# First loads by k-tile, the residual stream later, and a smaller-grained end in a two-layer fp32 trunk on one NeuronCore

## The chip, the cores and the metric

The kernel runs on one core of a Trainium2 chip. The metric is the device time in microseconds (us), lower is better. A run of the profiler gives, beside it, a trace of one execution; TensorE appears there as PE (matmuls) and PEld (weight loads), VectorE as DVE, ScalarE as ACT, GpSimd as POOL, SyncE, which issues most DMAs, as SP.

## The reference

Two layers over 256 tokens of width 1024, all in fp32. Cut to what matters:

```python
def rms_norm(x, g):
    return x * lax.rsqrt(jnp.mean(x * x, axis=-1, keepdims=True) + 1e-6) * g

def swiglu(x, w_in, w_out):                  # w_in 1024 x 5632, w_out 2816 x 1024
    gate, up = jnp.split(x @ w_in, 2, axis=-1)
    return (jax.nn.silu(gate) * up) @ w_out

h = x                                        # 256 x 1024
for i in range(2):
    h = h + 0.5 * swiglu(rms_norm(h, ffn_norm[i, 0]), ffn_w_in[i, 0], ffn_w_out[i, 0])
    u = rms_norm(h, mix_norm[i])
    h = h + (mla_mixer(u) if i == 0 else fox_mixer(u))
    h = h + 0.5 * swiglu(rms_norm(h, ffn_norm[i, 1]), ffn_w_in[i, 1], ffn_w_out[i, 1])
    gate = jax.nn.sigmoid(rms_norm(h, ple_norm[i]) @ ple_w_gate[i])
    h = h + gate * (p[i] @ ple_w_proj[i])
return rms_norm(h, final_norm)
```

## The kernel before

The residual stream lies in SBUF transposed, as `hT`: 8 k-tiles of 128 features by 256 tokens, in one tile `state` together with all norm gains (`g_sb`). Every weight and every activation that goes into a large product is split into a high part (rounded to fp32r) and a low part (the rest): ACT makes the high part (`whi`, lines 98 and 275), DVE the low part (`wlo`, lines 102 and 280). A product is then three fp32r products, hi·hi, hi·lo and lo·hi; `part` does them per k-tile with one matmul of 512 columns (both activation parts, line 236) and one of 256 (the low weights, line 237), `mm3` with three equal ones (lines 221 to 223), which is the form with the activations as the stationary operand.

`Weights` streams the weights in a fixed plan, in rows of 128 x 1024: a DMA on SP into one of four `raw` buffers, ACT and DVE into one of seven `whi`/`wlo` pairs, then PE. `pump` splits the next one and lets SP fetch into the buffer that this frees. All engines run their instructions in the written order.

RMSNorm is deferred: PE multiplies the gained but unnormalised stream, and the reciprocal root (`rtok`, on POOL, line 310, from `v` on DVE, line 308) is spread over the partitions by a small matmul (`by_column`, lines 315 and 318) and multiplied in when the product leaves PSUM (line 329). In the first FFN the sum of squares comes from a token-major copy of x, `tokens` (line 958 on ACT). There `ffn` puts `by_token` after the gate block of c = 2 and `by_column` after its up block; PE therefore takes the `pb` matmuls between the up block of c = 2 and the gate block of c = 3.

The start: SP loads `state` in three pieces (2, 2 and 4 k-tiles) alternating with four slabs of 128 x 1024 that hold the weights of the first two gate and up blocks, two k-tiles each; then two `raw`, the two halves of `tokens`, and two more `raw`. PE meanwhile runs 22 matmuls on zeros (`cold`). ACT and DVE split each k-tile's stream and weights in turn, and `first` multiplies k-tile by k-tile into four PSUM banks, each bank's 512-column matmul followed by its 256-column one.

The end is `ple_by_token`: the last gated embedding with tokens on the partitions, so that the final norm needs no transpose. For each of two token tiles t, two half rows of 512. The first halves of both are done together; then t = 0's second half (512), then t = 1's in two parts of 256 columns. After each part `gated` does sigmoid (ACT), two products and a sum (DVE), a square with row sum (ACT), and the product with the final gain (DVE, line 847). `store` adds the sums (853), scales and adds eps (854), takes the power on POOL (855), scales the row in two halves (858 ACT, 860 DVE) and stores them (861).

Of the kernel before, what the change touches and what calls it, by code (L numbers as in the profile page):

```python
# [60 lines left out]
class Weights:  # L61
# [20 lines left out]
    def take(self, raws):  # L82

        self.raws.update(enumerate(raws))
        self.fetched = self.ahead = len(raws)
# [56 lines left out]
def trunk(ctx, tc, xT, xt, pT, pos, freq, bf, ffn_first, ffn_in, ffn_out, w_down, w_uq, w_ukv, mla_o,  # L142
# [13 lines left out]
    def plan_ffn(i):  # L156

        plan.extend(ffn_first[k] for k in range(0 if i else KD // 2))
# [103 lines left out]
    class Norm:  # L262


        def __init__(self, gain, blocks, dim, tag="u"):
            self.gain, self.dim, self.acc, self.sums = gain, dim, None, None
            self.pair = act.tile([P, blocks, 2, T], F32R, name=tag, bufs=2 if tag == "u" else 1)

        def high(self, b, src, vector=False, cuts=(slice(0, T),)):
            g = g_sb[:, self.gain + b:self.gain + b + 1]  # L270
            for c in cuts:
                if vector:
                    nc.vector.tensor_scalar(self.pair[:, b, 0, c], src[:, c], g, None, op0=ALU.mult)
                else:
                    nc.scalar.activation(self.pair[:, b, 0, c], src[:, c], AF.Copy, scale=g)  # L275

        def low(self, b, src, cuts=(slice(0, T),)):
            g = g_sb[:, self.gain + b:self.gain + b + 1]
# [43 lines left out]
    def ffn(norm, nxt, then=None, first=None, meanwhile=None, later=None):  # L322
# [23 lines left out]
        def up(c, ps, pumps=1):  # L346
# [480 lines left out]
    def ple_by_token(pp, norm):  # L827
# [6 lines left out]
        sums = work.tile([P, 2, 3], F32, name="sums", bufs=1)  # L834
# [5 lines left out]
        def gated(t, ps, a, i):  # L840
# [5 lines left out]
            nc.scalar.activation(sg, h[:, t, a], AF.Square, accum_out=sums[:, t, i:i + 1])  # L846
            nc.vector.tensor_mul(es[:, t, a], h[:, t, a], gain[:, a])

        def store(t, n):
            s = work.tile([P, 1], F32, name="s")  # L850
            v = work.tile([P, 1], F32, name="v1")
            r = work.tile([P, 1], F32, name="r")
            nc.vector.reduce_sum(s, sums[:, t, :n], axis=AX.X)
            nc.vector.tensor_scalar(v, s, 1.0 / D, EPS, op0=ALU.mult, op1=ALU.add)
            nc.gpsimd.tensor_tensor(r, v, mhalf[:, :1], op=ALU.pow)
            for i, a in enumerate(half):
                if t and i == 0:
# [39 lines left out]
        for t in range(2):  # L897

            cuts = [half[1]] if t == 0 else [slice(N, N + N // 2), slice(N + N // 2, D)]
            for i, a in enumerate(cuts):  # L900
                last = bank("ps", (P, a.stop - a.start))
                for k in range(KD):
                    b = (k % 2 - 1) * N
                    rows(last, ws[k // 2], norm.pair, k, slice(a.start + b, a.stop + b), t, KD - 1)
                gated(t, last, a, 1 + i)
                if (t, i) == (1, 0):
                    store(0, 2)
        store(1, 3)
# [3 lines left out]
    n0 = Norm(G_FFN, KD, D)  # L912
    slabs = big.tile([P, KD // 2 + 2, D], F32, name="slabs", tag="big")
    tokens = slabs[:, KD // 2:, :]
    W.take([slabs[:, i, :] for i in range(KD // 2)])

    a = 0
    for i, n in enumerate((2, 2, 4, 0)):
        if n:
            b = GAINS + (2, 4, 8)[i] * T  # L920
            nc.sync.dma_start(state[:, a:b], xT[:, a:b])
            a = b
        nc.sync.dma_start(slabs[:, i, :], ffn_first[i])
# [4 lines left out]
    W.fetch()  # L928

# [3 lines left out]
    for _ in range(22):  # L933
        nc.tensor.matmul(cold, warm[:, :P], warm, start=True, stop=True)
    half = [slice(0, 4 * P), slice(4 * P, 8 * P)]
    for k in range(KD):
        if k % 2 == 0:
            W.pair()
        n0.high(k, hT[:, k, :])
        W.high(k // 2, half[k % 2])  # L940
        n0.low(k, hT[:, k, :])
        W.low(k // 2, half[k % 2])
# [3 lines left out]
    def first(ps):  # L946
        for k in range(0, KD, 2):
            w, = W.get()
            for j in range(2):
                for i, p in enumerate(ps):  # L950
                    part(p, w, n0.pair, range(k + j, k + j + 1), KD - 1, at=lambda x: (j * 4 + i) * P)
            W.done(w)
            W.pump()
            if k == 0:
# [143 lines left out]
def _layout(x, p, positions, ffn_norm, ffn_w_in, ffn_w_out, mix_norm, mla_w_down, mla_q_norm, mla_w_uq,  # L1098
# [58 lines left out]
_ORDER = ["xT", "xt", "pT", "pos", "freq", "bf", "ffn_first", "ffn_in", "ffn_out", "w_down", "w_uq", "w_ukv", "mla_o",  # L1157
# [22 lines left out]
```

## Time and profile before

| | us |
|---|---|
| median of 3 runs | 1001.4 (1001.32 to 1002.94) |
| the profiled execution | 1001.46 |
| its span, first to last instruction | 999.7 |
| PE busy in it | 988.8 (99%) |
| DVE, ACT, POOL busy | 740.5, 517.6, 423.7 |

Between the span and the time of the same execution lie 1001.46 - 999.7 = 1.8 us that no instruction shows. PE is busy for all but 11 us, so what is of interest is where those 11 us lie and what releases PE there. In the stretch from 24 to 960 us PE is busy for 934.5 of 936; the rest is in the first 24 us and in the 7.9 us after the last matmul.

### The profile page before, as it was taken

How to read it: one execution, taken by the hardware profiler on the slowest of the kernel's cores; microseconds unless marked ns; L12 is line 12 of the kernel's file. 1: busy time of each engine (PE TensorE's matmuls, PEld its weight loads, DVE VectorE, ACT ScalarE, POOL GpSimd, SP SyncE). 2: the span in 40 equal slices, each digit the busy share in tenths (PEclk: the TensorE clock that was granted, in tenths of full speed). 3: DMA queues.
4: the chain of work that ended last, by engine and by line, in shares of the span. 5: the costliest groups of instructions: out<-in, count | busy, mean ns of one | idle time of the engine just before them, and what ended most of it. 6: DMA issues, size and time to landing. Idle time of an engine off the chain costs nothing.

```text
span 999.7 us, 16018 instructions
## 1 busy us (share of the span) xinstructions
PE 988.8 (99%) x5940; PEld 875.1 (88%) x5940; DVE 740.5 (74%) x1051; ACT 517.6 (52%) x825; POOL 423.7 (42%) x348
## 2 busy tenths in 40 slices
PE   9999999999999999999999999999999999999996
PEld 7888888998988888889888888899889888888886
DVE  5777879676768787667778876666777778876674
ACT  7555444456655544555555444546445554544552
POOL 0777730110267775111477673211221577671120
PEclk9999999999999999999999999999999999999999
DMA  8566666651456666665366656666443566666561
GB/s 330 177 209 208 190 181 191 187 169 53 132 182 207 189 190 185 193 196 195 127 198 206 192 182 192 180 194 206 151 142 102 189 202 199 189 179 201 178 210 43
DMA packets 51388, 180.54 MB, mean 181 GB/s; under 512 B 5872, under 2 KB 6000, under 8 KB 51312
## 3 DMA queue, kind: packets, MB, share of 16 engines
q1 hardware_dynamic: 50880, 178.75, 57.3%
q8 instruction: 47, 0.77, 0.3%
q10 hardware_dynamic: 432, 0.79, 0.3%
q14 instruction: 29, 0.24, 0.1%
HBM read 178.46 MB, written 1.05 MB: 180 GB/s over the span
## 4 chain that ended last, share of the span: by engine, by line
PE 91%; DVE 4%; ACT 2%; issue 1%; POOL 0%; DMA 0%; POOLq 0%; SPq 0%; ACTq 0%; DVEq 0%
PE pu L236 16%; PE po L236 16%; PE pg L236 16%; PE po L237 8%; PE pu L237 8%; PE pg L237 8%; PE ps L236 4%; PE ps L237 2%; DVE wlo L102 1%; PE ps L221 1%; PE ps L223 1%; PE ps L222 1%; PE pv L221 1%; PE pv L223 1%; PE pv L222 1%
## 5 line engine op out<-in xcount | busy, mean ns | idle before, releaser
L102 DVE TENSOR_TENSOR wlo<-raw,whi 128x1024 fp32r<-128x1024 f32 (+2 forms) x338 | 416.8, 1241 | 17.8 <-ACT whi L98 17.1
L98 ACT ACTIVATE whi<-raw 128x1024 fp32r<-128x1024 f32 (+2 forms) x338 | 336.4, 1027 | 20.9 <-DMA raw<-in_ffn_in_dram 12.9
L331 POOL TENSOR_TENSOR gu<-two 128x256 f32<-128x256 f32 x176 | 235.5, 1339 | 117.9 <-DVE two L329 108.4
L236 PE MATMUL pg<-u,whi 128*128 128x512 f32 x704 | 251.7, 395 | 0.8 <-ACT whi L98 0.4
L236 PE MATMUL pu<-u,whi 128*128 128x512 f32 x704 | 251.1, 395 | 0.0
L236 PE MATMUL po<-hs,whi 128*128 128x512 f32 x704 | 246.0, 394 | 0.0
L237 PE MATMUL pg<-u,wlo 128*128 128x256 f32 x704 | 198.2, 282 | 0.3 <-DVE wlo L102 0.2
L237 PE MATMUL po<-hs,wlo 128*128 128x256 f32 x704 | 198.1, 281 | 0.0
L237 PE MATMUL pu<-u,wlo 128*128 128x256 f32 x704 | 198.0, 281 | 0.0
L236 PEld LDWEIGHTS pg<-u,whi 128*128 128x128 f32 x704 | 132.2, 188 | 32.1 <-DVE u L280 1.3
L236 PEld LDWEIGHTS pu<-u,whi 128*128 128x128 f32 x704 | 132.2, 188 | 30.3
L236 PEld LDWEIGHTS po<-hs,whi 128*128 128x128 f32 x704 | 132.2, 188 | 30.2
L237 PEld LDWEIGHTS pg<-u,wlo 128*128 128x128 f32 x704 | 132.5, 188 | 0.9 <-DVE wlo L102 0.9
L237 PEld LDWEIGHTS pu<-u,wlo 128*128 128x128 f32 x704 | 132.5, 188 | 0.0
L237 PEld LDWEIGHTS po<-hs,wlo 128*128 128x128 f32 x704 | 132.5, 188 | 0.0
L291 POOL TENSOR_TENSOR acc<-acc,sq 128x256 f32<-128x256 f32 x42 | 46.0, 1094 | 173.7 <-ACT sq L286 173.5
L213 ACT ACTIVATE hs<-hid 128x256 fp32r<-128x256 f32 x88 | 36.8, 418 | 142.1 <-POOL hid L349 140.1
L349 POOL TENSOR_TENSOR hid<-sg,gu 128x256 f32<-128x256 f32 x88 | 105.2, 1196 | 7.0 <-POOL gu L331 0.2
L217 DVE TENSOR_TENSOR hs<-hid,hs 128x256 fp32r<-128x256 f32 x88 | 63.5, 721 | 48.6 <-ACT hs L213 48.6
L329 DVE TENSOR_TENSOR two<-pg,rb 128x512 f32<-128x512 f32 x88 | 60.3, 685 | 46.8 <-PE pg L237 38.9
L275 ACT ACTIVATE u<-state 128x256 fp32r<-128x256 f32 x57 | 29.0, 509 | 125.7 <-DVE state L392 104.3
L343 ACT ACTIVATE sg<-gu 128x256 f32<-128x256 f32 x88 | 36.8, 418 | 78.5 <-POOL gu L331 78.5
(247 smaller groups left out, 1189.2 us busy)
## 6 DMA issues: line engine op xcount, KB each, us to landing
raw<-in_ffn_in_dram SPq DMA_DIRECT2D x172, 512.0 KB, 4.1
raw<-in_ffn_out_dram SPq DMA_DIRECT2D x64, 512.0 KB, 3.6
raw<-in_ffn_out_dram SPq DMA_DIRECT2D x32, 384.0 KB, 3.7
raw<-in_fox_qk_dram SPq DMA_DIRECT2D x16, 512.0 KB, 3.5
raw<-in_mla_o_dram SPq DMA_DIRECT2D x8, 512.0 KB, 4.4
raw<-in_ple_gate_dram SPq DMA_DIRECT2D x8, 512.0 KB, 4.6
raw<-in_fox_o_dram SPq DMA_DIRECT2D x8, 512.0 KB, 3.7
raw<-in_ple_rows_dram SPq DMA_DIRECT2D x8, 512.0 KB, 4.7
```

Of the source, the lines that this page charges most:

```text
L98: self.nc.scalar.activation(self.pairs[i][0][:, c], self.raws[i][:, c], AF.Copy)
L102: self.nc.vector.tensor_sub(lo[:, c], self.raws[i][:, c], hi[:, c].bitcast(F32))
L213: nc.scalar.activation(hi, src, AF.Copy)
L217: nc.vector.tensor_sub(lo, src, hi.bitcast(F32))
L236: nc.tensor.matmul(ps, hi, x[:, k], start=k == 0, stop=False)
L237: nc.tensor.matmul(ps[:, 1, :], lo, x[:, k, 0, :], start=False, stop=k == last)
L275: nc.scalar.activation(self.pair[:, b, 0, c], src[:, c], AF.Copy, scale=g)
L291: nc.gpsimd.tensor_add(new, self.acc, sq)
L329: nc.vector.tensor_mul(two, ps, norm.rb2)
L331: nc.gpsimd.tensor_add(gu[c, i], two[:, 0, :], two[:, 1, :])
L343: nc.scalar.activation(sg, gu.pop((c, 0)), AF.Silu)
L349: nc.gpsimd.tensor_mul(hid[c], gu.pop((c, 0)), gu.pop((c, 1)))
```

## The change

It has three parts.

1. **First loads.** The four slabs and three `state` pieces become eight rows `lead`, one per k-tile, each with that k-tile of the stream (256 columns) and its weights (512); the first also has the 16 gains that the first norm uses. They still go on SP's queue ahead of two `raw`, the tokens and two `raw`. The `cold` matmuls go from 22 to 18. For k-tile 0 the high part of the stream is made on DVE, and `first` does the four 512-column matmuls first and the four 256-column ones after them.
2. **The residual stream itself** (`state`, all 8 k-tiles and all gains, 128 x 2128) is loaded by one DMA that `up` issues at c = 8 of the first FFN, behind the `raw` loads that SP has by then.
3. **The end.** t = 1's second half is cut in 256, 128 and 128 columns in place of 256 and 256. All matmuls are issued ahead of the work on their results. The row sums are added as they come (`mean`, one DVE instruction per part in place of a reduction and a scaling at the end), the products with the gain are taken out of `gated` into `weigh`, and t = 1's row is scaled and stored as 384 columns by ACT and 640 by DVE and SP.

```diff
-            if (t, i) == (1, 0):
-                    store(0, 2)
-        store(1, 3)
+        cuts = [(0, N, D), (1, N, N + T), (1, N + T, N + T + P), (1, N + T + P, D)]
+        lasts = []
+        for i, (t, a, b) in enumerate(cuts):
+            lasts.append(bank("ps", (P, b - a)))
+            for k in range(KD):
+                o = (k % 2 - 1) * N
+                rows(lasts[i], ws[k // 2], norm.pair, k, slice(a + o, b + o), t, KD - 1)
+        cuts = [(t, slice(a, b)) for t, a, b in cuts]
+        gated(0, lasts[0], half[1], 1)
+        weigh(0, half[1])
+        mean(0, 1)
+        root(0)
+        gated(1, lasts[1], cuts[1][1], 1)
+        store(0, [(nc.vector, a) for a in half])
+        mean(1, 1)
+        gated(1, lasts[2], cuts[2][1], 2)
+        weigh(1, cuts[1][1])
+        mean(1, 2)
+        gated(1, lasts[3], cuts[3][1], 3)
+        weigh(1, slice(N + T, D))
+        mean(1, 3)
+        root(1)
+        c = N - P
+        store(1, [(nc.scalar, slice(0, c)), (nc.vector, slice(c, D))])
...
+        def mean(t, i):
+
+            v = work.tile([P, 1], F32, name="v1", bufs=4)
+            nc.vector.tensor_scalar(v, sums[:, t, i:i + 1], 1.0 / D, means[t], op0=ALU.mult, op1=ALU.add)
+            means[t] = v
...
+            if first and c == 8:
+
+                nc.sync.dma_start(state, xT)
...
-        nc.sync.dma_start(slabs[:, i, :], ffn_first[i])
+    nc.sync.dma_start(lead[:, :2 * KD + ROW], lead0)
+    for k in range(1, KD):
+        nc.sync.dma_start(steps[:, k, :], lead1[k - 1])
...
-    for _ in range(22):
+    for _ in range(18):
...
+        n0.high(k, steps[:, k, :T], vector=k == 0)
+        nc.scalar.activation(hi[:, c], steps[:, k, T:], AF.Copy)
+        n0.low(k, steps[:, k, :T])
+        rest(hi[:, c], lo[:, c], steps[:, k, T:])
...
+        for i, p in enumerate(ps):
+            nc.tensor.matmul(p, w[1][:, i * P:(i + 1) * P], n0.pair[:, 0], start=True, stop=False)
+        for i, p in enumerate(ps):
+            nc.tensor.matmul(p[:, 1, :], w[2][:, i * P:(i + 1) * P], n0.pair[:, 0, 0, :], start=False, stop=False)
```

Where instructions move, engine by engine. PE at the start, from the last `cold` matmul on; `u` is the split stream, `pg` and `pu` are the banks of the first two gate and up blocks. Before:

```order
L934 MATMUL cold_112<-warm_110 128x256
L236 MATMUL pg_185<-u_91,whi_135 128x512 [waits DVE_49,Activation_49]
L237 MATMUL pg_185<-u_91,wlo_136 128x256 [waits DVE_49]
L236 MATMUL pu_186<-u_91,whi_135 128x512
L237 MATMUL pu_186<-u_91,wlo_136 128x256
L236 MATMUL pg_187<-u_91,whi_135 128x512
```

and now:

```order
L958 MATMUL cold_113<-warm_111 128x256
L974 MATMUL pg_182<-u_110,whi_132 128x512 [waits DVE_49,Activation_49]
L974 MATMUL pu_183<-u_110,whi_132 128x512
L974 MATMUL pg_184<-u_110,whi_132 128x512
L974 MATMUL pu_185<-u_110,whi_132 128x512
L976 MATMUL pg_182<-u_110,wlo_133 128x256 [waits DVE_49]
```

The first wait for the low weights stands behind four matmuls in place of one.

DVE in the same stretch, from the split of the last k-tile of the start to the norm's `v`. Before:

```order
L102 TENSOR_TENSOR wlo<-slabs,whi 128x512 [waits Activation_49]
L102 TENSOR_TENSOR wlo<-raw,whi 128x1024 [waits DMAHW7_49,Activation_49]
L102 TENSOR_TENSOR wlo<-raw,whi 128x1024 [waits DMAHW0_49,Activation_49]
L102 TENSOR_TENSOR wlo<-raw,whi 128x1024 [waits DMAHW3_49,Activation_49]
L102 TENSOR_TENSOR wlo<-raw,whi 128x1024 [waits DMAHW4_49,PE_49,Activation_49]
L308 TENSOR_SCALAR v<-sums 128x2
```

and now:

```order
L216 TENSOR_TENSOR wlo<-lead,whi 128x512 [waits Activation_49]
L101 TENSOR_TENSOR wlo<-raw,whi 128x1024 [waits DMAHW0_49,Activation_49]
L101 TENSOR_TENSOR wlo<-raw,whi 128x1024 [waits DMAHW1_49,Activation_49]
L101 TENSOR_TENSOR wlo<-raw,whi 128x1024 [waits DMAHW4_49,Activation_49]
L101 TENSOR_TENSOR wlo<-raw,whi 128x1024 [waits DMAHW5_49,PE_49,Activation_49]
L308 TENSOR_SCALAR v<-sums 128x2
```

Nothing moved here: `v` still stands behind the split of the fourth `raw` row.

DVE at the end, from the product of t = 1's part of 256 columns. Before:

```order
L844 TENSOR_TENSOR sgr<-fin,sgr 128x256 [waits Activation_49]
L845 TENSOR_TENSOR fin<-fin,sgr 128x256 [waits DVE_49]
L847 TENSOR_TENSOR fin<-fin 128x256 [waits DVE_49]
L853 TENSOR_REDUCE s<-sums 128x1 [waits Activation_49]
L854 TENSOR_SCALAR v_10692<-s 128x1 [waits DVE_49]
L860 TENSOR_SCALAR fin<-fin,r 128x512 [waits Pool_49]
```

(this is the last part), and now:

```order
L847 TENSOR_TENSOR sgr<-fin,sgr 128x128 [waits Activation_49]
L848 TENSOR_TENSOR fin<-fin,sgr 128x128 [waits DVE_49]
L852 TENSOR_TENSOR fin<-fin 128x256 [waits DVE_49]
L857 TENSOR_SCALAR v_10725<-sums,v_10717 128x1 [waits Activation_49]
L865 TENSOR_SCALAR fin<-fin,r 128x640 [waits Pool_49]
```

The last part is half as wide, and the reduction is gone from behind its sum. On PE the 24 last matmuls of 256 columns have become 48 of 128, with the same 48 stationary operands loaded anew for each part.

## Rows read from the trace of the kernel before

**Rows 1.** The page: busy time of the engines, and the chain of work that ended last, by engine.

```profile
PE 988.8 (99%) x5940; PEld 875.1 (88%) x5940; DVE 740.5 (74%) x1051; ACT 517.6 (52%) x825; POOL 423.7 (42%) x348
...
PE 91%; DVE 4%; ACT 2%; issue 1%; POOL 0%; DMA 0%; POOLq 0%; SPq 0%; ACTq 0%; DVEq 0%
```

**Rows 2.** The timeline of ACT from 0 to 24 us: start, duration (us), engine, line, operation, tiles, and in brackets the idle time before it and what ended it.

```profile
3.59 0.51 ACT L275 ACTIVATE u<-state 128x256 fp32r<-128x256 f32 x1 [1.36 <-DMA state<-in_xT_dram]
5.66 0.63 ACT L98 ACTIVATE whi<-slabs 128x512 fp32r<-128x512 f32 x1 [1.57 <-DMA slabs<-in_ffn_first_dram]
...
6.60 0.61 ACT L98 ACTIVATE whi<-slabs 128x512 fp32r<-128x512 f32 x1
...
7.90 0.63 ACT L98 ACTIVATE whi<-slabs 128x512 fp32r<-128x512 f32 x1 [0.29 <-DMA slabs<-in_ffn_first_dram]
...
10.87 0.63 ACT L98 ACTIVATE whi<-slabs 128x512 fp32r<-128x512 f32 x1 [0.77 <-DMA slabs<-in_ffn_first_dram]
...
19.79 1.06 ACT L98 ACTIVATE whi<-raw 128x1024 fp32r<-128x1024 f32 x1 [0.26 <-DMA raw<-in_ffn_in_dram]
```

**Rows 3.** The timeline of DVE from 0 to 24 us, and then POOL's one instruction there.

```profile
6.32 0.69 DVE L102 TENSOR_TENSOR wlo<-slabs,whi 128x512 fp32r<-128x512 f32 x1 [1.71 <-ACT whi L98]
6.93 0.48 DVE L280 SCALAR_TENSOR_TENSOR u<-state,u 128x256 fp32r<-128x256 f32 x1
...
19.57 2.54 DVE L102 TENSOR_TENSOR wlo<-raw,whi 128x1024 fp32r<-128x1024 f32 x2 [1.96 <-ACT whi L98]
22.03 0.16 DVE L308 TENSOR_SCALAR v<-sums 128x2 f32<-128x2 f32 x1
...
22.34 0.71 POOL L310 TENSOR_TENSOR rtok<-v,mhalf 128x2 f32<-128x2 f32 x1 [20.85 <-DVE v L308]
```

**Rows 4.** The timeline of PE and PEld from 0 to 24 us: the `cold` matmuls, the first matmuls on data, the first of the gate block of c = 2 (at 18.14) and the weight loads of `by_column`.

```profile
1.08 4.87 PE L934 MATMUL cold<-warm 128*128 128x256 bf16 x22 [1.08 <-DVE warm L931]
6.34 0.50 PE L236 MATMUL pg<-u,whi 128*128 128x512 f32 x1 [0.39 <-ACT whi L98]
7.07 0.39 PE L237 MATMUL pg<-u,wlo 128*128 128x256 f32 x1 [0.23 <-DVE wlo L102]
7.30 0.40 PE L236 MATMUL pu<-u,whi 128*128 128x512 f32 x1
7.54 0.28 PE L237 MATMUL pu<-u,wlo 128*128 128x256 f32 x1
...
18.14 0.39 PE L236 MATMUL pg<-u,whi 128*128 128x512 f32 x1
...
23.63 0.53 PEld L315 LDWEIGHTS pb<-ident,rtok 128*128 128x128 f32 x4
```

**Rows 5.** The middle of the first FFN: what ACT's weight splits waited for from 24 to 140 us in all (us, times, longest); ACT's timeline at 73 us, when the row after the one that stands ahead of the moved load is split; busy times from 60 to 70 us (the last two figures are the DMA share and GB/s).

```profile
ACT whi L98 <- DMA raw<-in_ffn_in_dram: 0.2, 1, 0.2
...
73.35 2.00 ACT L98 ACTIVATE whi<-raw 128x1024 fp32r<-128x1024 f32 x2
...
60.00:70.00 10.00, 10.00 (x60) 8.74 (x59) 7.84 (x11) 5.50 (x9) 7.79 (x7) 1.00 0.67 218
```

**Rows 6.** The timeline of the end, from 986 us. PE's row at 986.17 is the first of the first part of 256 columns, that at 989.01 the first of the second, that at 991.74 the last of all.

```profile
986.17 0.28 PE L221 MATMUL ps<-whi,u 128*128 128x256 f32 x1
...
986.37 0.69 ACT L843 ACTIVATE sgr<-ps,rtok 128x512 f32<-128x512 f32 x1 [1.17 <-PE ps L223]
...
987.09 0.69 DVE L844 TENSOR_TENSOR sgr<-fin,sgr 128x512 f32<-128x512 f32 x1 [1.92 <-ACT sgr L843]
...
989.01 0.28 PE L221 MATMUL ps<-whi,u 128*128 128x256 f32 x1
...
991.74 0.28 PE L223 MATMUL ps<-wlo,u 128*128 128x256 f32 x1
...
992.12 0.47 ACT L843 ACTIVATE sgr<-ps,rtok 128x256 f32<-128x256 f32 x1 [0.97 <-PE ps L223]
...
992.78 0.42 DVE L844 TENSOR_TENSOR sgr<-fin,sgr 128x256 f32<-128x256 f32 x1
...
993.69 0.42 ACT L846 ACTIVATE sgr<-fin 128x256 f32<-128x256 f32 x1 [1.10 <-DVE fin L845]
...
994.23 0.16 DVE L853 TENSOR_REDUCE s<-sums 128x1 f32<-128x3 f32 x1
...
995.24 0.72 ACT L858 ACTIVATE fin<-fin,r 128x512 f32<-128x512 f32 x1 [1.04 <-POOL r L855]
995.24 0.48 DVE L860 TENSOR_SCALAR fin<-fin,r 128x512 f32<-128x512 f32 x1 [0.67 <-POOL r L855]
996.00 0.35 ACTq L861 DMA_DIRECT2D out_dram<-fin  x1
```

**Rows 7.** Weight loads: four for a product of one moving column, with the next load of PEld behind them (timeline, 964 us); then groups by shape (busy us, mean ns): a bf16 load, the loads of the `mm3` products that the end consists of, and the f32 loads of the one-column products.

```profile
964.46 0.53 PEld L305 LDWEIGHTS pst<-ones,acc 128*128 128x128 f32 x4 [0.16 <-POOL acc L291]
964.91 0.19 PEld L221 LDWEIGHTS pe<-whi,q 128*128 128x128 f32 x1
...
L549 PEld LDWEIGHTS <-identb 128*128 128x128 bf16 x16 | 1.6, 98 | 0.4
L221 PEld LDWEIGHTS ps<-whi,u 128*128 128x128 f32 x40 | 7.5, 188 | 1.0
L305 PEld LDWEIGHTS pst<-ones,acc 128*128 128x128 f32 x32 | 4.2, 190 | 0.9 <-ACT rb L318 0.7 <-POOL acc L291 0.2
```

More of the change, by code (lines that the diff above doesn't have):

```diff
@@ L80, in raw, with skip @@
         return raw, src
-    def take(self, raws):
-        self.raws.update(enumerate(raws))
-        self.fetched = self.ahead = len(raws)
+    def skip(self, n):
+        self.fetched = self.ahead = n
     def fetch(self):
@@ L156, in plan_ffn @@
     def plan_ffn(i):
-        plan.extend(ffn_first[k] for k in range(0 if i else KD // 2))
+        plan.extend(ffn_in[0, c] for c in range(0 if i else KD // 2))
         plan.extend(ffn_in[i, c] for c in range(0 if i else 4, 2 * KF))
@@ L277, in low @@
         def low(self, b, src, cuts=(slice(0, T),)):
-            g = g_sb[:, self.gain + b:self.gain + b + 1]
+            g = self.g[:, b:b + 1]
             for c in cuts:
@@ L833, in ple_by_token @@
         half = [slice(0, N), slice(N, D)]
-        sums = work.tile([P, 2, 3], F32, name="sums", bufs=1)
+        sums = work.tile([P, 2, 4], F32, name="sums", bufs=1)
         def rows(ps, w, x, k, a, t, last):
@@ L896, in ple_by_token @@
             gated(t, ps[t], half[0], 0)
[L897 to L905, printed above, removed]
-                if (t, i) == (1, 0):
-                    store(0, 2)
@@ L908, in ple_by_token @@
-        store(1, 3)
-        W.done(*ws)
[L912 to L922, printed above, removed]
-        nc.sync.dma_start(slabs[:, i, :], ffn_first[i])
+            weigh(t, half[0])
@@ new lines, in ple_by_token @@
+            mean(t, 0)
+        cuts = [(0, N, D), (1, N, N + T), (1, N + T, N + T + P), (1, N + T + P, D)]
[8 more added lines that the diff above has]
+        weigh(0, half[1])
@@ new lines, in ple_by_token @@
+        mean(0, 1)
[12 more added lines that the diff above has]
+        store(1, [(nc.scalar, slice(0, c)), (nc.vector, slice(c, D))])
+        W.done(*ws)
+    ROW = T + 4 * P
+    lead = big.tile([P, 2 * KD + KD * ROW + 2 * D], F32, name="lead", tag="big")
@@ L928, in trunk @@
     W.fetch()
+    n0 = Norm(G_FFN, KD, D, table=lead)
     warm = const.tile([P, T], BF16, name="warm")
@@ L932, in trunk @@
     cold = bank("cold", (P, T))
-    for _ in range(22):
+    for _ in range(18):
         nc.tensor.matmul(cold, warm[:, :P], warm, start=True, stop=True)
-    half = [slice(0, 4 * P), slice(4 * P, 8 * P)]
     for k in range(KD):
         if k % 2 == 0:
[L938 to L942, printed above, removed]
+            hi, lo = W.pair()
+        c = slice(k % 2 * 4 * P, (k % 2 + 1) * 4 * P)
+        n0.high(k, steps[:, k, :T], vector=k == 0)
+        nc.scalar.activation(hi[:, c], steps[:, k, T:], AF.Copy)
+        n0.low(k, steps[:, k, :T])
+        rest(hi[:, c], lo[:, c], steps[:, k, T:])
         if k % 2:
@@ L946, in first @@
     def first(ps):
[L947 to L954, printed above, removed]
+        w, = W.get()
+        for i, p in enumerate(ps):
+            nc.tensor.matmul(p, w[1][:, i * P:(i + 1) * P], n0.pair[:, 0], start=True, stop=False)
+        for i, p in enumerate(ps):
+            nc.tensor.matmul(p[:, 1, :], w[2][:, i * P:(i + 1) * P], n0.pair[:, 0, 0, :], start=False, stop=False)
+        for k in range(1, KD):
+            if k % 2 == 0:
+                w, = W.get()
+            for i, p in enumerate(ps):
+                part(p, w, n0.pair, range(k, k + 1), KD - 1, at=lambda x: (k % 2 * 4 + i) * P)
+            if k % 2:
+                W.done(w)
+                W.pump()
+            if k == 1:
                 n0.sums = const.tile([P, 2], F32, name="sums")
```

44 lines of the change are left out of this document (24 added, 20 removed).

## The prediction

> **What bounds the kernel now.** I read the page first: PE is busy for 99% and is 91% of the chain that ended last [rows 1]. So a change can only win where PE waits, which the time table puts at the two ends, and it can lose wherever it gives PE more to do. Then the timelines of the two ends, engine by engine.
>
> At the start PE has its first data matmul at 6.34 and waits once more until 7.07; from 7.30 on it runs without a break: 31 pairs of a 512- and a 256-column matmul lie between 7.30 and the gate block of c = 2 at 18.14, 0.35 us a pair, 1.40 us a k-tile of four pairs [rows 4]. What PE waited for is ACT, and ACT waited for the first slab, landed at 5.66 [rows 2]. That is the first place.
>
> The second place does not show as a wait. `by_column` loads `rtok` into PE at 23.63 [rows 4], and POOL had `rtok` only at 22.34 + 0.71 = 23.05 [rows 3]. Back from there: `v` on DVE at 22.03, the split of the fourth raw row on DVE, its high part on ACT at 19.79, for which ACT waited for a DMA [rows 2, 3]. So 0.58 us behind PE runs a chain that the landing of the fourth raw row sets, and that row lands when everything ahead of it on SP's queue has landed.
>
> At the end PE starts its last matmul at 991.74; from then on every step waits for the one before it, until the last stores are issued at 996.00 and the span ends at 999.7 [rows 6].
>
> **The start, first matmul.** Landings by bytes: 296 KB at 3.59, 808 KB at 5.66, 1576 KB at 7.90, 2600 KB at 10.87 and 6184 KB (the fourth raw row) at 19.79 [rows 2], so 247, 343, 345 and 402 KB/us. The first lead row has 392 KB, each further one 384. Read off between those points, k-tiles 0, 1 and 2 land at 4.0, 5.5 and 6.7, the last at 12.1. For k-tile 0, ACT needs 0.63 for the high weights, until 4.65; DVE makes the stream's two parts in 0.35 (an estimate below the 0.48 of its other pass) + 0.48, until 4.85, and the low weights in 0.69 more, until 5.6 [rows 2, 3]. The 18 cold matmuls at 4.87/22 = 0.22 each end at 5.05, so PE turns to data at about 5.0. Their 0.22 for 256 columns is the 1.2 GHz level; the 0.24 from 7.30 to 7.54 for 512 columns is the 2.4 GHz level [rows 4], and when between it rose the rows leave open. At the low level four 512-column matmuls take 1.7 us, at the high one 0.95; k-tile 0 is through between 6.4 and 7.2. It doesn't matter which: k-tile 1's low weights come later still. ACT has them from 5.5: stream 0.5, weights until 6.6; DVE then 0.48 for the stream's low part and 0.69 for the weights', until about 7.3. PE therefore waits there to 7.3, does the rest of k-tile 1 (0.12 + 3 x 0.35) to 8.5 and waits no more: ACT's pace is 0.94 a k-tile (5.66 to 6.60), DVE's 1.2, the landings' 0.95 to 1.1, all under 1.40. The gate block of c = 2 starts at 8.5 + 6 x 1.40 = 16.9 in place of 18.14: **1.24 us ahead**, with 0.4 as a worst case if the low weights of k-tile 1 come 0.8 later.
>
> **The start, what is left of it.** `by_column` would be reached at 23.63 - 1.24 = 22.39. But the chain to `rtok` doesn't move with it: on DVE `v` stays behind the fourth raw row, as the order of the change shows, and the bytes ahead of that row shrink only by 32 KB of 6184, 0.08 us. `rtok` is ready at 22.97, PE takes it some 0.06 later, so PE waits some 0.65 us and goes on 23.63 - 23.03 = 0.60 us ahead of before; I take **0.55 gained** of the 1.24. Bounds: 1.24, if the fourth row lands 0.7 earlier than I read; 0 or a loss, if it lands over 0.6 later.
>
> Against eight loads of 392 and 384 KB there speaks a rule of the Trainium skill, page "DMA: Bandwidth & Descriptors", section "Rules for kernel authors": for most bandwidth, 128 partitions and at least 1 MiB a DMA. By the rows a mixture of 256 and 512 KB pieces (5.66 to 7.90) ran as fast as two of 512 KB (7.90 to 10.87), 343 and 345 KB/us, so the trace doesn't bear it out where several transfers are queued; by the rule the rows would come later, which is the slow rival below.
>
> **The middle.** The load of 128 x 2128 (1064 KB) is in SP's order behind a raw row and ahead of the next, whose split ACT begins at 73.35 with no wait. At 402 KB/us it holds the queue for 2.6 us. The cover: ACT is idle for 4.5 of 10 us there and DVE for 2.2, ACT's splits waited 0.2 us for DMA in all from 24 to 140 [rows 5], and `catch_up` keeps four split rows, 4 x 2.75 = 11 us of PE work (a block is half of 18.14 to 23.63), ahead of PE. Without that cover it would cost up to 2.6; nothing can be gained. I take 0. Nobody reads `state` before the down projection of that FFN.
>
> **The end, PE.** The part of 256 columns from 986.17 to 989.01 has 24 matmuls, 0.118 us each, and the last of 256 starts its last one 2.73 us later [rows 6]. Now 48 of 128 columns stand in the place of 24. Does a matmul of 128 columns take half of one of 256? Each loads its own 128 x 128 fp32r weights, and no row shows one under 256 columns. The nearest: four f32 loads for products of one column take 0.53 with the last one's 0.19 in it, (0.53 - 0.19)/3 = 0.113 us apart, though the product itself is next to nothing; and the loads of the products at the end take 188 ns, like those f32 ones with 190, where a bf16 load takes 98 [rows 7]. So the load sets the pace: 0.113 each. Upper bound 0.118 (as with 256 columns), lower bound 0.059 (half of that). The last matmul then starts at 989.01 + 47 x 0.113 = 994.32: **2.58 us later** (2.8 by the upper bound, 0.05 by the lower).
>
> **The end, behind PE.** From the last matmul to the scaling of the row before: 995.24 - 991.74 = 3.50 us. Half the columns save: 0.06 in the matmul; 0.11 in the sigmoid (half of the step 0.69 to 0.47 from 512 to 256); 0.13 in each of two DVE passes (half of 0.69 to 0.42, a little less for starts); 0.11 in the square with its sum; the reduction, 0.16 and its gap, 0.19; and DVE was held by the stores of t = 0 until 992.78 with the sigmoid done at 992.59, 0.15 [rows 6]. Sum 0.06 + 0.11 + 0.26 + 0.11 + 0.19 + 0.15 = 0.88. The last scaling: ACT's 384 columns 0.1 shorter than 0.72, DVE's 640 0.06 longer than 0.48, and SP's last store 64 KB larger; I take the later of the two and the sum of bytes as before: 0. With the products by the gain beside ACT's square, not behind it, nothing is added there. So the end moves by 2.58 - 0.88 = +1.70; I take **+1.6** (ACT's shorter pass counts in part), bounds +1.4 and +2.0 as long as the load sets the pace.
>
> **Sum.** Against the profiled execution: 1001.46 - 0.55 + 1.6 = 1002.5; its own time stands 0.06 over the median of the three, so 1002.5 - 0.06, rounded **1002.4**.
>
> **Rivals.**
>
> *The narrow matmuls keep up.* If loads overlap fully, 0.059 each, the last matmul starts at 991.78 and the end wins 0.04 - 0.88 = -0.84: 1001.4 - 0.55 - 0.84 = 1000.0. For it: PE overlaps loads with matmuls all through. Against it: the f32 loads at 0.113 with nothing to hide behind, and 188 against 98 ns [rows 7]. The Trainium skill, page "TensorE: Matmul & The Clock Gate", section "Back-to-back issue gap", has about 81 ns for load and matmul of 128 columns; at that pace the sum would be 989.01 + 47 x 0.081 = 992.82, +1.08 - 0.88 - 0.55, about 1001.1. Its section on weight-path modes leaves fp32 out of the fast load, which goes with the row. Chance of a pace clearly under 0.1: 13 in 100, 1000.0 to 1001.1.
>
> *The chain to `rtok` comes along.* If the queue delivers the fourth raw row 0.7 us earlier, the whole 1.24 stays: 1001.4 - 1.24 + 1.6 = 1001.8. For it: SP issues the raw rows earlier. Against: they were already queued long before; the pace of 402 KB/us [rows 2] is that of a full queue. 8 in 100.
>
> *Slower: the lead rows arrive at a lower pace.* If loads with 3 KB rows ran at the 247 KB/us of the first stretch, the seven later ones would take 10.9 us after 4.0, the last landing at 14.9 in place of 12.1, the fourth raw row 2.8 later, and PE would stand at `by_column` until 25.8, a loss of 2.2 in place of the gain: 1001.4 + 2.2 + 1.6 = 1005.2. It decides from about 310 KB/us on, where the start gains nothing. Against it: the pieces of 256 KB among slabs at 343 [rows 2]. 7 in 100.
>
> **How the numbers follow.** The forecast has 72 in 100; its own range, 1001.5 to 1003.4, comes from the pace of 0.109 to 0.118, a start between +0.2 and -1.0 and some 0.2 of difference between runs. The range for 8 in 10 takes in the quicker end of the first rival and leaves out its far end and the slow rival: 1000.8 to 1003.5. A measurement of this kernel can tell about 0.2%, 2 us, from no change: faster than 999.4 needs the first two rivals at once, 3 in 100; slower than 1003.4 is the slow rival and the upper edge of the forecast, 13; the rest, 84, is no change that can be told.
>
> **What would show it.** Right: first data matmul near 5.0 and the gate block of c = 2 near 16.9; then a wait of PE at `pb` for POOL of about 0.6, with `pb` near 23.1; no PE wait near 75 us; 48 weight loads at the end 0.11 apart; from the last matmul to the scaling about 2.6. Wrong: loads 0.06 apart there, `pb` reached without a wait, or ACT waiting for lead rows past k-tile 2.

## The result and the profile after

| | before | after |
|---|---|---|
| median, us | 1001.38 (1000.83 to 1003.13, 20 runs) | 1003.01 (1002.27 to 1004.58, 20 runs) |
| the profiled execution | 1001.46 | 1003.04 |
| its span | 999.7 | 1001.2 |
| PE busy | 988.8 | 990.8 |

The ratio after to before is 1.0014, with a 95% interval of 1.0008 to 1.0021: about 1.5 us slower, within the 0.2% that the prediction called no change that can be told. The start won a little and the end lost more than that.

The page of the kernel after: busy times and the chain by engine, to be read beside [rows 1]. PE does 2.0 us more, with 20 more matmul records (48 in place of 24 at the end, 4 fewer `cold` ones).

```profile
PE 990.8 (99%) x5960; PEld 877.2 (88%) x5960; DVE 741.6 (74%) x1056; ACT 517.8 (52%) x827; POOL 424.6 (42%) x348
...
PE 89%; DVE 4%; ACT 2%; issue 2%; DMA 2%; POOL 1%; SPq 0%; POOLq 0%; ACTq 0%; DVEq 0%
```

**The start.** ACT of the kernel after, from 0 to 24 us (start, duration, engine, line, operation, tiles, idle before and what ended it), to be read beside [rows 2]: its four waits for `lead` rows, and the split of the fourth `raw` row.

```profile
3.94 0.63 ACT L964 ACTIVATE whi<-lead 128x512 fp32r<-128x512 f32 x1 [1.72 <-DMA lead<-in_lead_dram]
5.22 0.51 ACT L275 ACTIVATE u<-lead 128x256 fp32r<-128x256 f32 x1 [0.65 <-DMA lead<-in_lead_dram]
...
6.60 0.51 ACT L275 ACTIVATE u<-lead 128x256 fp32r<-128x256 f32 x1 [0.35 <-DMA lead<-in_lead_dram]
...
8.34 0.51 ACT L275 ACTIVATE u<-lead 128x256 fp32r<-128x256 f32 x1 [0.70 <-DMA lead<-in_lead_dram]
...
19.87 1.06 ACT L97 ACTIVATE whi<-raw 128x1024 fp32r<-128x1024 f32 x1 [0.27 <-DMA raw<-in_ffn_in_dram]
```

PE, PEld and POOL of the same stretch, beside [rows 3, 4]: the end of `cold`, the data matmuls of k-tile 0, the first two waits, the gate block of c = 2, and `by_column`.

```profile
1.08 4.01 PE L958 MATMUL cold<-warm 128*128 128x256 bf16 x18 [1.08 <-DVE warm L955]
4.96 0.47 PE L974 MATMUL pg<-u,whi 128*128 128x512 f32 x1
5.27 0.39 PE L974 MATMUL pu<-u,whi 128*128 128x512 f32 x1
...
7.04 0.38 PE L236 MATMUL pg<-u,wlo 128*128 128x256 f32 x1 [0.17 <-DVE wlo L216]
...
9.69 0.40 PE L235 MATMUL pg<-u,whi 128*128 128x512 f32 x1
10.14 0.39 PE L236 MATMUL pg<-u,wlo 128*128 128x256 f32 x1
...
17.05 0.39 PE L235 MATMUL pg<-u,whi 128*128 128x512 f32 x1
...
22.30 0.19 PEld L236 LDWEIGHTS pu<-u,wlo 128*128 128x128 f32 x1
23.19 0.52 PEld L315 LDWEIGHTS pb<-ident,rtok 128*128 128x128 f32 x4 [0.71 <-POOL rtok L310]
...
22.43 0.71 POOL L310 TENSOR_TENSOR rtok<-v,mhalf 128x2 f32<-128x2 f32 x1 [20.94 <-DVE v L308]
```

PE starts on data at 4.96 and reaches the gate block of c = 2 at 17.05 in place of 18.14, 1.09 ahead. At `by_column` PEld then stands idle for 0.71 and goes on when POOL is done (22.43 + 0.71 = 23.14): a wait where [rows 4] had none. What is left of 1.09 is 23.63 - 23.19 = 0.44.

**The middle.** SP's and ACT's timelines around the moved load, beside [rows 5]: the load goes out at 64.90, and ACT splits the next rows with no wait for a DMA.

```profile
64.90 0.42 SPq L355 DMA_DIRECT2D state<-in_xT_dram  x1
...
72.89 1.04 ACT L97 ACTIVATE whi<-raw 128x1024 fp32r<-128x1024 f32 x1
```

**The end**, beside [rows 6]: the first matmul of the part of 256 columns, the first two of 128 columns, the last of all, and what follows it.

```profile
985.94 0.28 PE L220 MATMUL ps<-whi,u 128*128 128x256 f32 x1
...
988.79 0.22 PE L220 MATMUL ps<-whi,u 128*128 128x128 f32 x1
988.85 0.27 PE L221 MATMUL ps<-whi,u 128*128 128x128 f32 x1
...
993.98 0.27 PE L222 MATMUL ps<-wlo,u 128*128 128x128 f32 x1
...
994.35 0.37 ACT L846 ACTIVATE sgr<-ps,rtok 128x128 f32<-128x128 f32 x1 [1.23 <-PE ps L222]
...
996.13 0.55 POOL L870 TENSOR_TENSOR r<-v,mhalf 128x1 f32<-128x1 f32 x1 [6.22 <-DVE v L857]
996.72 0.61 ACT L863 ACTIVATE fin<-fin,r 128x384 f32<-128x384 f32 x1 [0.91 <-POOL r L870]
...
997.36 0.35 ACTq L866 DMA_DIRECT2D out_dram<-fin  x1
```

From the first to the last of these matmuls it is 993.98 - 985.94 = 8.04 us, before 991.74 - 986.17 = 5.57: +2.47. The 128-column ones stand 0.111 apart (988.85 to 993.98 in 46 steps), hardly closer than those of 256 columns (0.118). Behind the last matmul the tail is shorter: 997.36 - 993.98 = 3.38 to the last issue, before 996.00 - 991.74 = 4.26, so -0.88. Of these, 0.76 lie ahead of the scaling of the row (996.72 - 993.98 = 2.74, before 995.24 - 991.74 = 3.50), and 0.11 are ACT's scaling itself, of 384 columns in place of 512 (0.61, before 0.72). From the last issue to the span's end it is 1001.2 - 997.36 = 3.8, before 3.7.

The account by these rows: -0.23 (PE's lead when the part of 256 begins) + 2.47 - 0.88 + some 0.2 (stores) = +1.56. The spans differ by 1.5, the times of the two profiled executions by 1.58.

### The profile page after: what moved, and what is told of

Its sections match the earlier page's. It is cut to its first block, busy times and chain, and to the rows that moved or that the text cites. A ratio compares the mean times of both kernels' runs of the same rounds, so it can differ in the third digit from the quotient of the medians.

```text
span 1001.2 us, 16069 instructions
## 1 busy us (share of the span) xinstructions
PE 990.8 (99%) x5960; PEld 877.2 (88%) x5960; DVE 741.6 (74%) x1056; ACT 517.8 (52%) x827; POOL 424.6 (42%) x348
## 3 DMA queue, kind: packets, MB, share of 16 engines
HBM read 179.52 MB, written 1.05 MB: 180 GB/s over the span
## 4 chain that ended last, share of the span: by engine, by line
PE 89%; DVE 4%; ACT 2%; issue 2%; DMA 2%; POOL 1%; SPq 0%; POOLq 0%; ACTq 0%; DVEq 0%
PE po L235 16%; PE pu L235 16%; PE pg L235 15%; PE po L236 8%; PE pu L236 8%; PE pg L236 8%; PE ps L235 4%; PE ps L236 2%; DVE wlo L101 1%; PE ps L222 1%; PE ps L220 1%; PE ps L221 1%; DMA raw<-in_ffn_in_dram 1%; PE pv L220 1%; PE pv L222 1%
## 5 line engine op out<-in xcount | busy, mean ns | idle before, releaser
L275 ACT ACTIVATE u<-state 128x256 fp32r<-128x256 f32 x49 | 25.0, 510 | 123.2 <-DVE state L395 102.9
```

## The experiments

### The two halves alone

The start alone: the kernel after with `ple_by_token` of the kernel before.

```diff
-        cuts = [(0, N, D), (1, N, N + T), (1, N + T, N + T + P), (1, N + T + P, D)]
...
+            cuts = [half[1]] if t == 0 else [slice(N, N + N // 2), slice(N + N // 2, D)]
```

> The change's first loads and its later load of the residual stream, with the end of the kernel before. My theory (the start gains some 0.5 us because PE, though 1.2 us ahead, then waits at the norm's small matmul for a chain that hangs on the landing of the fourth raw row): about 1000.9 us against 1001.4 of before, PE waiting 0.7 us for POOL at pb near 23.2, and the last matmul 0.2 to 0.5 us earlier than before. Rival (the later load or the smaller loads cost something in the middle that eats the start): 1001.4 or more, with a PE wait between 60 and 140 us.

Measured: 1001.28 us, ratio 0.9995 (0.9986 to 1.0004), `pb` at 23.11. In time it can't be told from the kernel before. The trace shows the wait for `rtok` (0.47) and a lead of 0.52 at `pb`, of which 0.32 is left at the last matmul (991.42, before 991.74): the start is worth 0.3 to 0.5 us, too little to show in the time.

The end alone: the kernel before with `ple_by_token` of the kernel after (the same diff, its signs turned round). It was run twice.

> The change's end alone, on the start of before. My theory (each of the 48 last matmuls takes the 0.11 us of its weight load, so PE ends 2.5 us later, and 0.9 comes back behind it): 1003.0 us, 1.6 over before, weight loads 0.11 us apart in the last 5.3 us. Rival (the narrow matmuls are not what costs; the whole sum comes from the start or the middle): 1000.5 to 1001.4.

> The kernel before with the new end alone, a second time, for its last stores: 4.7 us from their issue to the span's end where all other kernels with that end took 3.85, and a median 1.2 over what the sum of the terms gave. If that was a trait of one run (theory), it is 3.85 here and the time 1.6 over the kernel before. If it belongs to the kernel (rival), 4.7 again and 2.7 over.

Measured: 1004.25 us, ratio 1.0026 (1.0018 to 1.0035), and again 1003.95, ratio 1.0024 (1.0014 to 1.0034). So the end is what costs, but by 2.5, not by 1.6. The 0.9 more stands in the last stores. The rows are the profile's last line on DMA issues, for the kernel after and then for the first of these two: KB, and median us from issue to landing.

```profile
out_dram<-fin ACTq DMA_DIRECT2D x1, 192.0 KB, 2.6
```

```profile
out_dram<-fin ACTq DMA_DIRECT2D x1, 192.0 KB, 3.5
```

The same store of the same size lands 0.9 later in this kernel, in both runs, and in no other kernel here. I had expected a trait of one run; it is one of the kernel. One thing goes with it in all 14 profiles: in these two runs a packet of 8 KB on a queue that the profile calls "instruction" begins while the last stores are on their way (at 999.59 and 1000.30 us), and in none of the others does one begin between their issue and their landing. The row is the first run's, from 997 to 1002.5 us: queue, packets, MB, share.

```profile
q14 instruction: 1, 0.01, 0.4%
```

Whether that packet delays the store was not tested, so the cause stays open.

### The wait for rtok: which chain holds the lead back

In the kernel after the root was taken earlier: `by_token` of the first norm behind the split of the second `raw` row, so that `v` on DVE doesn't stand behind the fourth.

```diff
+            if k == 3:
+                n0.by_token()
+                n0.rooted = True
...
-                norm.by_token()
+                if not norm.rooted:
+                    norm.by_token()
```

> The changed kernel with one step moved: v and rtok of the first norm are computed right behind the split of the second raw row on DVE, not behind that of the fourth. My theory (the chain through the fourth raw row holds PE at pb): rtok is ready near 19.5, PE reaches pb near 22.4 without a wait, 0.7 us under the changed kernel, so 1002.3 against its 1003.0, 0.9 over before. Rival (something else paces the start, such as the k-tiles' splits): pb is reached no earlier and the time stays at 1003.0.

Measured: 1002.41 us, ratio 1.0007 (0.9998 to 1.0016). POOL's root and PE's loads in its timeline:

```profile
18.73 0.71 POOL L310 TENSOR_TENSOR rtok<-v,mhalf 128x2 f32<-128x2 f32 x1 [17.24 <-DVE v L308]
...
22.43 0.53 PEld L315 LDWEIGHTS pb<-ident,rtok 128*128 128x128 f32 x4
```

The root is there 3.0 us before PE comes, the loads begin without a wait, and PE is 23.63 - 22.43 = 1.20 ahead. So the rest of the start's gain was indeed held by that chain. In the time it is 0.6 us under the kernel after by the medians, with intervals that overlap, so it is the trace that shows it.

The control is the same edit in the kernel before, where PE came later than the root.

```diff
+            if k == 2:
+                n0.by_token()
+                n0.rooted = True
```

> The kernel before, with the first norm's root taken as soon as the third raw row has been split, not behind the fourth. In the kernel before, PE reached the four pb loads at 23.63 without a wait, rtok being ready at 23.05. If the chain to rtok only matters for a PE that is ahead of it (my theory), nothing is won here: pb at 23.6 again, 1001.4 us as the kernel before, within 0.3. Rival: the earlier root itself is worth something (it frees DVE or POOL earlier), as much as the variant of the changed kernel with it won, 0.6 us: 1000.8.

Measured: 1001.64 us beside 1001.84, ratio 0.9992 (0.9984 to 1.0001), in its timeline:

```profile
18.14 0.71 POOL L310 TENSOR_TENSOR rtok<-v,mhalf 128x2 f32<-128x2 f32 x1 [16.65 <-DVE v L308]
...
23.54 0.53 PEld L315 LDWEIGHTS pb<-ident,rtok 128*128 128x128 f32 x4
```

`rtok` is 4.2 us earlier than in [rows 3] and `pb` where it was, by 0.1. An earlier root wins nothing where nobody waits for it.

### The end: columns or weight loads

One wider part: the last two parts of 128 columns as one of 256, all else as in the kernel after.

```diff
-        cuts = [(0, N, D), (1, N, N + T), (1, N + T, N + T + P), (1, N + T + P, D)]
+        cuts = [(0, N, D), (1, N, N + T), (1, N + T, D)]
...
-        gated(1, lasts[3], cuts[3][1], 3)
-        weigh(1, slice(N + T, D))
-        mean(1, 3)
```

> The changed kernel with the last two parts of 128 columns made one of 256; everything else of the new end (matmuls issued first, sums added as they come, 384 and 640 columns at the last scaling) stays. My theory: PE's last matmul comes 2.5 us earlier, the tail behind it is 0.4 us longer (its passes are twice as wide), so 2.0 us under the changed kernel: 1000.9 us, 0.5 under before. Rival (the new order of the work on the results costs, not the width): about 1003.

Measured: 1000.99 us, ratio 0.9991 (0.9983 to 1.0). Its last matmul and its last issue:

```profile
991.75 0.28 PE L222 MATMUL ps<-wlo,u 128*128 128x256 f32 x1
...
995.62 0.35 ACTq L866 DMA_DIRECT2D out_dram<-fin  x1
```

From the one to the other it is 3.87, 0.39 less than before (4.26) with the same 256 columns. About 0.1 of it is ACT's scaling of 384 columns in place of 512 (0.62 and 0.72); the rest, some 0.3, is what the sums made as they come and the new order of DVE's work are worth. The narrower part's own share of the 0.88 is 0.49, and its price is 2.47.

One narrower part: the last 128 columns as 64 and 64.

```diff
-        cuts = [(0, N, D), (1, N, N + T), (1, N + T, N + T + P), (1, N + T + P, D)]
+        cuts = [(0, N, D), (1, N, N + T), (1, N + T, N + T + P), (1, N + T + P, N + T + P + 64), (1, N + T + P + 64, D)]
...
+        gated(1, lasts[4], cuts[4][1], 4)
+        weigh(1, slice(N + T, D))
+        mean(1, 4)
```

> The changed kernel with its last part of 128 columns cut into 64 and 64, so 24 more matmuls, each with its own 128 x 128 weight load. If the load sets the pace whatever the columns (theory), 72 matmuls stand 0.112 apart where 48 did, the last matmul moves by 24 x 0.112 = 2.7 us, the work behind it on half the columns saves some 0.3 to 0.4: about 1005.3 us. Rival: a matmul of 128 columns costs 0.112 by its columns, one of 64 half of that: 48 of them at 0.056, the last matmul where it was, the tail 0.3 shorter: 1002.7.

Measured: 1007.53 us, ratio 1.0052 (1.0037 to 1.0068); the profiled execution was its fastest, 1005.96. Its PE around 995 us:

```profile
995.25 0.28 PE L222 MATMUL ps<-wlo,u 128*128 128x64 f32 x1
995.36 0.36 PE L220 MATMUL ps<-whi,u 128*128 128x64 f32 x1
995.54 0.40 PE L221 MATMUL ps<-whi,u 128*128 128x64 f32 x1
995.76 0.40 PE L222 MATMUL ps<-wlo,u 128*128 128x64 f32 x1
```

and the windows of the 128-column part, of the 64-column parts up to there, and of what follows (busy time and instructions of PE, PEld, DVE, ACT and POOL, then the granted clock, DMA share and GB/s):

```profile
988.41:990.93 2.52, 2.52 (x26) 2.52 (x24) 2.20 (x7) 1.19 (x5) 0.55 (x1) 1.00 0.00 0
991.04:995.25 4.21, 4.21 (x40) 4.21 (x40) 1.63 (x7) 1.43 (x6) 0.00 (x0) 1.00 0.33 125
995.36:997.04 1.68, 1.68 (x11) 1.68 (x10) 0.05 (x1) 0.00 (x0) 0.00 (x0) 0.52 0.00 0
```

Matmuls of 64 columns stand 0.11 apart as well: a quarter of the columns of 256, and nearly the same time (0.118 there). The price is per matmul and its load, whatever the matmul's columns: the column theory is out. That it is the load, and not a fixed price of every such pair, no run tested by itself, but rows of another product in the kernel after speak for the load. Two matmuls with bf16 operands, each behind a load of its own, stand 0.06 apart, and a bf16 load takes 98 ns where one of these takes 188 [rows 7]:

```profile
702.03 0.22 PE L767 MATMUL psc<-drop,pick 96*128 96x128 bf16 x1
702.09 0.27 PE L767 MATMUL psc<-drop,pick 96*128 96x256 bf16 x1
```

The Trainium skill, page "TensorE: Matmul & The Clock Gate", section "LDWEIGHTS (loading the stationary operand)", lets a load's time go by the columns of the stationary operand alone, by its formula an estimated 107 ns for 128; the trace agrees in the size, with 0.111 from one load to the next.

The run shows more than was expected. At 995.36 the granted clock falls from 1.00 to 0.52, from the 2.4 to the 1.2 GHz level, and the step from one matmul to the next doubles to 0.21, though PE and PEld count as busy all the time and nothing is waited for. The last eight matmuls cost 0.1 each on top; without these 0.8 the profiled execution would stand at 1005.2, where the load theory put it. The other three executions of this kernel took 1007.00 to 1008.31; whether they lost the clock earlier isn't shown, as none of them was profiled.

### The moved load

The load of `state` twice in a row, into the same tile, so that SP's queue stands for the first landing and then carries 1064 KB once more.

```diff
                 nc.sync.dma_start(state, xT)
+                nc.sync.dma_start(state, xT)
```

> The changed kernel with the moved load of the residual stream issued twice in a row into the same tile, so that SP's queue stands for the first one's landing and then carries 1064 KB more. If that load is free because rows split ahead cover it (theory: 11 us of PE work ahead), PE still has no wait from 60 to 140 us and the time is that of the changed kernel, 1003.0 within 0.4; ACT or DVE may wait for a raw row once. Rival: the cover is thin, and a queue held for some 6 to 8 us instead of 2.6 shows as a PE wait for a split row: 1005 to 1008.

Measured: 1003.27 us, ratio 1.0012 (1.0002 to 1.0021), as the kernel after. SP's timeline, and then what ACT waited for from 24 to 140 us (us in total, times, longest):

```profile
65.08 0.42 SPq L355 DMA_DIRECT2D state<-in_xT_dram  x1
71.23 0.33 SPq L356 DMA_DIRECT2D state<-in_xT_dram  x1
```

```profile
ACT whi L97 <- DMA raw<-in_ffn_in_dram: 5.2, 2, 4.3
```

The queue was held 6 us longer, ACT stood for a `raw` row for 4.3 us, and in the same stretch PE has no wait at all. The rows split ahead cover the load with room to spare; the zero for the moved load is right, and for the reason given.

### The start's rows, and a pause far behind

The six last `lead` rows in three loads of 768 KB:

```diff
-    for k in range(1, KD):
-        nc.sync.dma_start(steps[:, k, :], lead1[k - 1])
+    nc.sync.dma_start(steps[:, 1, :], lead1[0])
+    for k in range(2, KD, 2):
+        nc.sync.dma_start(steps[:, k:k + 2, :], lead1[k - 1:k + 1].rearrange("k p n -> p k n"))
```

> The changed kernel with its six last lead rows loaded as three DMAs of 768 KB in place of six of 384. The rule that larger DMAs move more would have the rows land earlier; by the rows of this case a pair lands when its second row did, so the first of each pair waits up to 1.0 longer for the same bytes. Theory: k-tile 2 is split about 1 us later, PE waits there some 0.5 to 1.0 more, is less ahead at pb, and the wait for rtok hides most of that: pb at 23.1 to 23.6, 1003.0 to 1003.4. Rival: the larger DMAs land as early as the single rows did, and PE reaches k-tile 2 with no more wait: 1003.0 with pb at 23.1, the fourth raw row earlier than 19.6.

Measured: 1003.81 us, ratio 1.0023 (1.0014 to 1.0033). ACT's second and third wait there, and PE's for k-tile 2:

```profile
5.14 0.51 ACT L275 ACTIVATE u<-lead 128x256 fp32r<-128x256 f32 x1 [0.58 <-DMA lead<-in_lead_dram]
...
9.10 0.51 ACT L275 ACTIVATE u<-lead 128x256 fp32r<-128x256 f32 x1 [2.93 <-DMA lead<-in_lead_dram]
...
10.27 0.47 PE L235 MATMUL pg<-u,whi 128*128 128x512 f32 x1 [1.61 <-DVE u L280]
```

The first pair is there at 9.10, where the kernel after had the first of the two rows at 6.60 and the second at 8.34: the larger load was the later one even for its last byte. PE waits 1.61 and comes to `pb` at 24.66, behind the kernel before. My size for that wait, 0.5 to 1.0, was too small. By the ratios the kernel is 0.09% slower than the kernel after, with intervals that overlap, so this rests on the one profile.

The high part of the stream's k-tile 0 on ACT, so that DVE runs one instruction less at the start:

```diff
-        n0.high(k, steps[:, k, :T], vector=k == 0)
+        n0.high(k, steps[:, k, :T])
```

> The changed kernel with the high part of the stream's k-tile 0 on ACT, as all others, so that DVE runs one instruction less at the start, as in the kernel before. In every kernel with the new start DVE stands 0.35 us longer ahead of its product at 462 us (3.06 idle where 2.71), and PE loses as much behind it. If that pause hangs on the place in DVE's instruction stream (theory), it is gone here or has moved to where it costs nothing, and PE's lead at 485 us is that at 252 us. Rival: it comes from what the new start does to the DMA queue or the buffers; then 3.06 stays. For the time: k-tile 0 some 0.2 to 0.5 later, which the wait at pb hides: 1002.7 with the theory, 1003.0 with the rival.

Measured: 1002.97 us, ratio 1.0013 (1.0004 to 1.0022), with the pause still there (3.07). The pause is the idle time in brackets, of DVE ahead of its first product at 462 us. PE meets it at 485 us, where it waits 0.7 for DVE in place of 0.4 and its lead falls from 0.61 to 0.24. The rows are of the kernel after and of the one before, each with the matmul that the product waits for, and of the one with loads in pairs.

```profile
461.65 0.28 PE L222 MATMUL ps<-u,whi 128*128 128x256 f32 x1
462.39 0.42 DVE L791 TENSOR_TENSOR zg<-ps,rb 128x256 f32<-128x256 f32 x1 [3.06 <-PE ps L222]
```

```profile
462.26 0.28 PE L223 MATMUL ps<-u,whi 128*128 128x256 f32 x1
462.65 0.42 DVE L788 TENSOR_TENSOR zg<-ps,rb 128x256 f32<-128x256 f32 x1 [2.71 <-PE ps L223]
```

```profile
463.57 0.42 DVE L791 TENSOR_TENSOR zg<-ps,rb 128x256 f32<-128x256 f32 x1 [2.71 <-PE ps L222]
```

The bracket names PE, but PE had long been done: its matmul ends at 461.65 + 0.28 = 461.93 and the product begins 0.46 later, before 0.11 later (462.54 to 462.65). So it is DVE that pauses.

My theory was that the pause hangs on the place in DVE's instructions. The two runs look like its end, as the pause stays in the one with DVE's instruction taken away, and the one with pairs, which does the same work on DVE, hasn't got it. But DVE's waits for semaphores are instructions too, and with them counted the theory holds: 703 instructions stand ahead of the product in the nine profiles with the pause (3.06 to 3.08), and 702 or 700 in the five without (2.71 to 2.72). In the kernel above with all high parts on ACT one instruction went and one wait came, and with loads in pairs three waits went, so neither run put the theory to the test that I meant. Two more things go with the pause in all 14 profiles. One is the lead, with `pb` at 23.40 or earlier in the nine and at 23.54 or later in the five. The other is an 8 KB packet on that instruction queue, which begins between 459.2 and 460.2 us in the nine and in none of the five; the row is that of the kernel after, from 459 to 460.5 us.

```profile
q14 instruction: 1, 0.01, 2.7%
```

In the nine some 0.35 to 0.4 of PE's lead is lost, whatever its size. Which of the three is the cause stays open, as no run kept one and changed another.

### Both repairs together

The kernel after with the early root and the wide last part; then the same with the last scaling and stores cut at 512 columns.

```diff
-        c = N - P
+        c = N
```

> The changed kernel with both repairs: the first norm's root behind the second raw row's split, and the last two parts of 128 columns as one of 256. If the two places are independent, as the theory has it, the gains add: 1003.0 - 0.6 (root early, alone 1002.41) - 2.0 (wide end, alone 1000.99) = 1000.4 us, 0.9 to 1.0 under the kernel before; PE about 1.2 ahead of it after the start, some 0.3 of it lost near 462 us, last matmul near 990.8. Rival: PE ahead by more runs into another wait in the middle or at the end that takes the second gain back: 1000.9 to 1001.2, with that wait in PE's waits.

> The kernel with both repairs (root early, last part of 256 columns), its last scaling and stores cut at 512 columns as in the kernel before, not at 384. In the changed kernel the time from the last store's issue to the span's end was 3.84 us where the kernel before had 3.66; if the larger store of 640 columns on SP is the cause (theory), it comes back to 3.7, while ACT's scaling of 512 columns takes 0.1 longer: nothing in all, 0.1 either way. Rival: the 3.84 has another cause and stays; then 0.1 is lost. In the time both are under what can be told: 0.8 to 0.9 under the kernel before.

Measured: 1000.96 us beside 1001.84, ratio 0.9985 (0.9977 to 0.9994), and 1000.59 beside 1001.43, ratio 0.9985 (0.9976 to 0.9994). Both are faster than the kernel before by some 1.5 us by the ratio, 0.8 to 0.9 by the medians, and 2 to 3 us faster than the kernel after. From the last issue to the span's end the first took 3.9 and the second 3.7, so the 0.2 in the stores does hang on the larger store; in time the two can't be told apart. The gains add, less than fully in the first one's profile: `pb` at 23.09, 0.54 ahead in place of 1.2, since its `lead` rows were late, and no new wait of PE behind it.

## Why the prediction was right

- **First matmul and the lead at c = 2.** Predicted 5.0 and 16.9, 1.24 ahead; measured 4.96 and 17.05, 1.09 ahead. The rows landed at 3.94, 5.22 and 6.60 where 4.0, 5.5 and 6.7 were read off [rows 2]. That the lead comes within 0.15 is in part luck, as two errors offset each other: PE's wait for the low weights of k-tile 1 ended at 7.04, not 7.3, and the fourth row, at 8.34, was late, for which PE lost 0.33 (its lead falls from 1.44 to 1.11; one step of it is 9.69 to 10.14, where such a step takes 0.23). With loads in pairs, in their one profile, there was no lead at all.
- **What is left of it at pb.** Predicted a wait and 0.55; measured 0.44 here and 0.52 with the start alone. The mechanism is shown by the early root, which kept 1.20, and its control.
- **The middle.** Predicted 0 for the moved load: shown, with twice the load. What I didn't see is the pause of DVE at 462 us, because it is no wait in the kernel before. Of PE's lead of 0.44 it takes 0.37; 0.23 arrives at the end, as 0.17 were won at other places on the way.
- **The end on PE.** Predicted 0.113 a matmul and +2.58; measured 0.111 and +2.47. That the columns don't set the pace is shown by 64 columns in the same time; that the load does is argued from rows. The rival of 0.059 is out, and so is the 0.081 that the Trainium skill's page "TensorE: Matmul & The Clock Gate" has in its section "Back-to-back issue gap", for operands of this type. The prediction also said that no row shows a matmul under 256 columns, and one of the kernel before does: 16 f32 loads, each with a matmul of 128 columns, in 1.90 us, so (1.90 - 0.19)/15 = 0.114 apart. The price could have been read there.

```profile
967.56 1.90 PEld L879 LDWEIGHTS ph<-ident,state 128*128 128x128 f32 x16
```

- **Behind PE.** Predicted -0.88 up to the scaling of the row, measured -0.76 there (2.74, where 2.6 was forecast). Up to the last issue it is -0.88, with 0.11 from ACT's shorter scaling, for which the prediction had taken off 0.1 in going from +1.70 to +1.6. So the equal numbers stand for different stretches. Like for like the tail was taken 0.1 too short and PE's part 0.11 too long; that the end's sum comes out at 1.6 is in part luck. Nearly half of what was won has nothing to do with the narrower part, as the wide end shows: 0.39 of 0.88. The last stores, taken as 0, cost 0.2.
- **The sum.** In the profiled runs +1.05 was predicted and +1.58 measured. The 0.5 lies in the start and the pause (0.23 arrived in place of 0.55) and in the stores (0.2), not in the end's two large terms, whose sum of +1.59 stood as 1.6. By the medians the forecast of 1002.4 was 0.6 too low.

## What to carry to other kernels

Before a last product is cut finer, compare the step between its matmuls with that of narrower ones elsewhere in the trace, down to one column: here the step was 0.118 with 256 columns and 0.111 with 128 and with 64, so the cut from 256 to 128 cost 24 more loads and won back a fifth of their time behind PE. A start that begins earlier is worth only what the next chain lets through: look, before cutting, for what is ready less than the gain ahead of its reader, and move that chain too. And cut first loads by what the first reader needs: here, in the trace, larger loads came later for their first reader and also for their last byte.

## What was not expected of the hardware

- The granted clock fell from 1.00 to 0.52 while PE ran matmuls of 64 columns without a pause, after 4.3 us of them. With 128 columns, 5.2 us long, it didn't fall.
- A store of 192 KB took 3.5 us to land in the kernel with the new end alone, in both of its runs, and 2.6 to 2.7 in all others that have it.
- The same first loads land unevenly: in nine profiles with the same eight `lead` rows, k-tile 1 began to be split between 4.81 and 6.40 us, and `pb`, in the six of them without the earlier root, stood between 22.70 and 23.40.
- DVE paused 0.35 longer at 462 us in nine of 14 profiles. These are the ones with one to three more DVE instructions ahead of the product, with PE 0.2 us or more ahead, and with an 8 KB instruction packet that begins 2.3 to 3.0 us ahead of it.
